# Output projection of a decoder layer: the first three heads' weight blocks by seven block products, in a written-out order

## The chip, the cores and the metric

The kernel runs on one core of one Trainium2 chip. The time is device microseconds (us) from launch to end, the median of several runs. TensorE (PE) does the matrix products; VectorE (DVE), ScalarE (ACT) and GpSimd (POOL) work element by element; SyncE (SP) and ACT start transfers (DMA) between DRAM and on-chip memory.

## The reference

One decoder layer over 512 tokens of width 1024. A matrix-memory attention of four heads (256 columns each) and a causal convolution of width 31 give two halves of 1024 columns, which one output projection maps back; a gated convolutional feed-forward follows. The part that the change touches:

```python
h = mlstm_chunkwise(q, k, v, i_gate, f_gate)            # 4 heads x 256
h = rms_norm(h, ml_norm_g) * sigmoid(o_pre)
y = silu(layer_norm(causal_dwconv(a * sigmoid(gt))))    # 1024 channels
mix = concatenate([h, y], axis=-1) @ w_out[l]           # (512, 2048) @ (2048, 1024)
x = x + g1 * rms_norm(mix, mix_post_g[l])
u = rms_norm(x, ffn_pre_g[l]) * (1.0 + sc2) + sh2
```

All is float32. `sc2`, `sh2` and the gains come from 48 blocks of a conditioning product (`ada_w`).

## The kernel before, in words

**How a product is made.** Each float32 operand is split into a high part, rounded to the matmul's type, and a low part, the rest. `mm3` (the matmuls at L210) then takes three matmuls of 512 columns: high by high, high by low, low by high. Weights come by SP into two raw buffers of 128x2048 (`raws`, RAWS = 2); `w_split` makes the high part on ACT (L191) and the low part on POOL (L192), into 20 tiles (`wpool`, ten pairs). A raw buffer is loaded again when its last split is done, a pair when its last matmul is done.

**The stages.** The input projection, attention head by head (`attention`, with `make_vo` and `head_proj` of the next head between its steps), the output projection, the feed-forward up (`up`) and down (`dn`). The 31 convolution taps run on DVE beside the first half of the program. PE and SP follow the program text; for DVE, ACT and POOL a scheduler sets one order per engine, and each engine then takes its instructions strictly in that order. Inside `in_order()` their order is the program's too.

**The output projection.** 2048 rows of `w_out` are 16 row blocks of 128, of which two belong to each head (`hy[0]` to `hy[7]`) and eight to the convolution (`hy[8]` to `hy[15]`); 1024 columns are two halves of 512; 512 tokens are four tiles. `mix_first` adds the left half into four banks (`mixa`), block by block, between the steps of the last head's attention: scores `s` (L551), sums over values `o` (L562), a factor per token (`ssq`, `fac`, L576 to L581), scaled rows `hn` on ACT (L585), transposed as `hT` (L593), split into `hh` and `hl` (L599, L600). The right half goes into `mixb`: eight blocks for all tiles, and eight in `mix_last`, tile by tile. There a chain per token tile (`chain_sums`, `chain_x`, `chain_u`: L724 to L984) makes the normed row `un`, which PE transposes (`xT`, L992) for the up projection.

**Beside it.** `ada_block` (L176) loads 512 KB from the ACT queue and reduces it on DVE to one column of `mod` (tile `junk`); blocks 24 to 39 use four buffers in `spare` and two in `adas`, and give `sc2` and `sh2`, whose rows `gs2r` and `sh2r` the chain needs. A load into a used buffer waits, on ACT's own queue, for the DVE reduction that read it.

Of the kernel before, what the change touches and what calls it, by code (L numbers as in the profile page):

```python
# [22 lines left out]
H = 4  # L23
# [28 lines left out]
MIX = [*range(6), *range(8, 14), 6, 7, 14, 15]  # L52
# [3 lines left out]
def decoder_layer(ctx, tc, w_glu0, x, c, adaT, vecs, w_glu, w_qko, w_v0, w_vo, w_out, w_up, w_down, out):  # L56
# [111 lines left out]
    def ada_block(i, behind):  # L168
# [5 lines left out]
        nc.scalar.dma_start(r, adaT[i // 2][:, (i % 2) * D : (i % 2 + 1) * D])  # L174
# [51 lines left out]
    def rms_bcast(ps, n, scale, name, bank=atbank):  # L226
# [5 lines left out]
        return bcast(r, n, f"{name}_b", bank)  # L232

    def rms_factor(acc, n, scale, name):
        return rms_bcast(colsum(acc, n, f"{name}_s"), n, scale, name)
# [197 lines left out]

    def glu_gate(i):
# [55 lines left out]
    def make_vo(h):  # L490
# [50 lines left out]
    last_e = [None]  # L541

    def attention(h):
# [35 lines left out]
        G.tensor_tensor(out=fac, in0=ssq, in1=mhalf, op=ALU.pow)  # L579
# [9 lines left out]
        for e in range(2):  # L589
# [99 lines left out]
    def send_rows(a, n, queue=nc.scalar):  # L689
# [3 lines left out]
        t = (side if a == 3 * KT else slot)(f"gTs{a}")[:, :P]  # L693
# [38 lines left out]
    KA = 8  # L732

# [15 lines left out]

# [64 lines left out]
    def norm_mean():  # L814
# [7 lines left out]
        for j in range(KT):  # L822
            V.scalar_tensor_tensor(out=ys[j], in0=tot, scalar=-1.0 / D, in1=ys[j], op0=ALU.mult, op1=ALU.add)

    yr = []

    def norm_sums():
        yr.append(colsum(ysq, T, "ry_s", cvbank))

    def norm_rows():  # L830
        yr.append(rms_bcast(yr[0], T, 1.0 / D, "ry", cvbank))

    def norm_tiles(a, b):
        yb = yr[1]
        for j in range(a, b):
            V.tensor_tensor(out=ys[j], in0=ys[j], in1=yb, op=ALU.mult)
            S.activation(ys[j], ys[j], AF.Silu, bias=vcol("cv_ln_b", j), scale=vcol("cv_ln_g", j))
            hi, lo = slot(f"yh{j}", F32R), slot(f"yl{j}", F32R)
            S.activation(hi, ys[j], AF.Copy)
            V.tensor_tensor(out=lo, in0=ys[j], in1=hi.bitcast(F32), op=ALU.subtract)  # L840
            hy[KT + j] = (hi, lo)

    for h in range(H - 1):
        head_load(h + 1)
        steps = attention(h)
        if h == 0:
# [47 lines left out]

    tc.cur_priority += LATER
    for i in range(16, 20):
        ada_block(i, scaled)
    tc.cur_priority -= LATER
    wo = {}
    steps = attention(H - 1)  # L900
    next(steps)
    mix_first(0)
    next(steps)
    tc.cur_priority += LATER
    for i in range(20, 24):
        ada_block(i, last_e[0])
    ada_done(16, 24)
    gain(0, 16, "mix_post_g")
    tc.cur_priority -= LATER
    norm_rows()  # L910
    norm_tiles(0, 4)
    mix_first(1)
    mix_first(2)
    mix_first(3)
    mix_first(4)
    next(steps)
    norm_tiles(4, KT)
    mix_first(5)
    next(steps)
    mix_first(6)  # L920
    next(steps)
    for n in range(7, 10):
        mix_first(n)
    for _ in steps:
        pass
    spare.append(upool.tile([P, KT, T], F32, tag="ul", name="spare"))
    for i in range(24, 40):
        ada_block(i, last_lo[0])
    ada_done(24, 40)
    for n in range(10, 2 * KT):  # L930
        mix_first(n)
        if n == 10:
            send_rows(0, KT)
    mg = [slot(f"mg{tt}") for tt in range(NT)]
# [4 lines left out]
    for tt, ps in enumerate(mixa):  # L939
        V.tensor_tensor(out=mg[tt], in0=ps, in1=g1r[0], op=ALU.mult)  # L940
        sq_sum(ps, msq[:, 2 * tt : 2 * tt + 1], f"mixa{tt}")
    banks = [atbank(f"mixb{tt}") if tt < 2 else cvbank(f"mixb{tt}") for tt in range(NT)]
    for n_, k in enumerate(MIX[:KA]):
        if n_ % 4 == 0:
            wo = wo_rows(1, n_ // 4)
        for tt, ps in enumerate(banks):
            mm3(ps, (hy[k][0][:, tok(tt)], hy[k][1][:, tok(tt)]), wo[n_ % 4], n_ == 0, False)
# [431 lines left out]
```

## Time and profile before

| | |
|---|---|
| three runs | 769.36, 768.62, 769.15 us; median 769.15 us |
| span of the profiled execution (first to last instruction) | 767.4 us |
| median run less that span | 1.75 us |
| busy share of the span | PE 99%, DVE 75%, POOL 67%, ACT 54% |
| granted TensorE clock, mean | 0.999 |
| output projection, from the first `mixa` matmul to the last of `mixb` | 317.24 to 414.00 us |

The profile is one execution recorded by the hardware. A row of a timeline or of a chain begins with the start in us from the span's beginning and the duration; matmuls overlap, so that their pitch is smaller than their duration. "Idle before" is the time for which the engine had nothing to do, with what ended it. ACTq and SPq are the queues that start transfers.

### The profile page before, as it was taken

The page shows a single profiled execution, that of the slowest core. Times are in us where ns is not written, and L with a number is a line of the kernel's source. Part 1 is how long each engine was busy: PE and PEld are TensorE (multiplying, and loading weights), DVE is VectorE, ACT ScalarE, POOL GpSimd, SP SyncE. Part 2 cuts the span into 40 slices and gives each one's busy share as a digit, 9 for nine tenths or more (in the row PEclk, how much of TensorE's full clock was granted, in tenths as well). Part 3 has the DMA queues.
Part 4 walks back from the last instruction along what each step waited for, and adds up shares of the span by engine and source line. Part 5 has one row for each costly group of instructions (what it writes and reads, how often), then busy time and mean ns, then how long its engine had stood idle before and what let it go on. Part 6 is the DMA issues. An engine that isn't in the chain of part 4 may idle for free.

```text
span 767.4 us, 10129 instructions
## 1 busy us (share of the span) xinstructions
PE 756.0 (99%) x3480; PEld 625.1 (81%) x3480; DVE 576.6 (75%) x837; ACT 410.7 (54%) x778; POOL 516.5 (67%) x428
## 2 busy tenths in 40 slices
PE   7999999999999999999999999999999999999996
PEld 5778898878788788888889988888888888888885
DVE  6669999979979696476989978675684775654547
ACT  6675428585665655573345444443534444566633
POOL 4779849796494872645631179786887884599943
PEclk9999999999999999999999999999999999999999
DMA  8973313411131241655965755666767565796273
GB/s 317 349 281 113 112 56 117 158 56 56 55 111 56 98 168 64 235 199 168 365 222 183 271 210 191 240 219 247 262 231 275 187 239 185 271 397 241 93 249 135
DMA packets 40136, 147.32 MB, mean 192 GB/s; under 512 B 3826, under 2 KB 5266, under 8 KB 30484
## 3 DMA queue, kind: packets, MB, share of 16 engines
q1 hardware_dynamic: 27524, 96.59, 34.9%
q10 hardware_dynamic: 12560, 50.08, 18.3%
q8 instruction: 27, 0.44, 0.2%
q14 instruction: 25, 0.20, 0.1%
HBM read 126.59 MB, written 20.07 MB: 191 GB/s over the span
## 4 chain that ended last, share of the span: by engine, by line
PE 93%; DMA 4%; POOL 1%; ACT 1%; issue 0%; DVEq 0%; SPq 0%; DVE 0%; POOLq 0%; ACTq 0%
PE up L210 31%; PE dn L210 13%; PE qko L210 13%; PE vo L210 9%; PE glu L210 7%; PE mixa L210 6%; PE mixb L210 6%; DMA wglu<-in_w_glu 3%; PE o L562 2%; PE s L551 2%; PE v L210 2%; PE glu L350 1%; DMA xn<-in_x 1%; PE xT L992 0%; PE hT L593 0%
## 5 line engine op out<-in xcount | busy, mean ns | idle before, releaser
L774 DVE SCALAR_TENSOR_TENSOR cv<-gt,cvw,cv 128x485 f32<-128x485 f32 (+24 forms) x200 | 137.2, 731 | 2.1 <-ACT cv L762 0.8
L770 POOL TENSOR_TENSOR cs<-cs,cs 128x510 f32<-128x510 f32 (+3 forms) x32 | 42.1, 1316 | 0.2
L192 POOL TENSOR_TENSOR wup_0l<-wup,wup_0h 128x512 fp32r<-128x512 f32 x18 | 25.0, 1389 | 19.4 <-ACT wup_0h L191 19.3
L210 PE MATMUL up<-u2h,wup_0h 128*128 128x512 f32 (+1 forms) x96 | 35.8, 373 | 0.0
L210 PE MATMUL up<-u2h,wup_0l 128*128 128x512 f32 (+1 forms) x96 | 35.7, 371 | 0.0
L210 PE MATMUL up<-u2h,wup_512h 128*128 128x512 f32 (+1 forms) x96 | 35.6, 371 | 0.0
L210 PE MATMUL up<-u2l,wup_512h 128*128 128x512 f32 (+1 forms) x96 | 35.6, 371 | 0.0
L210 PE MATMUL up<-u2h,wup_512l 128*128 128x512 f32 (+1 forms) x96 | 35.6, 371 | 0.0
L210 PE MATMUL up<-u2l,wup_0h 128*128 128x512 f32 (+1 forms) x96 | 35.6, 371 | 0.0
L210 PE MATMUL up<-u2h,wup_1024h 128*128 128x512 f32 (+1 forms) x92 | 35.0, 381 | 0.0
L210 PE MATMUL up<-u2l,wup_1024h 128*128 128x512 f32 (+1 forms) x92 | 34.9, 380 | 0.0
L210 PE MATMUL up<-u2h,wup_1536l 128*128 128x512 f32 (+1 forms) x92 | 34.9, 380 | 0.0
L210 PE MATMUL up<-u2h,wup_1536h 128*128 128x512 f32 (+1 forms) x92 | 34.9, 380 | 0.0
L210 PE MATMUL up<-u2l,wup_1536h 128*128 128x512 f32 (+1 forms) x92 | 34.9, 380 | 0.0
L210 PE MATMUL up<-u2h,wup_1024l 128*128 128x512 f32 (+1 forms) x92 | 34.9, 380 | 0.0
L176 DVE SCALAR_TENSOR_TENSOR junk<-ada,cb 128x1024 bf16<-128x1024 f32 x20 | 29.9, 1493 | 2.6 <-DMA ada<-in_adaT 2.5
L768 ACT ACTIVATE cs<-gt,cvw 128x511 f32<-128x511 f32 (+4 forms) x40 | 27.1, 713 | 6.1 <-POOL cs L770 3.5
L192 POOL TENSOR_TENSOR wup_1536l<-wup,wup_1536h 128x512 fp32r<-128x512 f32 x18 | 24.6, 1365 | 6.0 <-ACT wup_1536h L191 5.4
L191 ACT ACTIVATE wup_512h<-wup 128x512 fp32r<-128x512 f32 x22 | 13.8, 629 | 25.7 <-PE up L210 20.9
L192 POOL TENSOR_TENSOR wup_1024l<-wup,wup_1024h 128x512 fp32r<-128x512 f32 x18 | 23.6, 1314 | 5.0 <-ACT wup_1024h L191 5.0
L330 DVE SCALAR_TENSOR_TENSOR junk<-ada,cps 128x1024 bf16<-128x1024 f32 x16 | 19.5, 1220 | 9.8 <-DMA ada<-in_adaT 9.2
L1113 DVE TENSOR_TENSOR b<-b 128x512 f32<-128x512 f32 x11 | 19.4, 1762 | 8.6 <-POOL b L1112 8.6
(1097 smaller groups left out, 2726.8 us busy)
## 6 DMA issues: line engine op xcount, KB each, us to landing
wup<-in_w_up SPq DMA_DIRECT2D x22, 1024.0 KB, 5.0
b<-in_w_down ACTq DMA_DIRECT2D x11, 1024.0 KB, 5.1
spill_t<-b ACTq DMA_DIRECT2D x11, 1024.0 KB, 3.9
ada<-in_adaT ACTq DMA_DIRECT2D x20, 512.0 KB, 4.8
wqko<-in_w_qko SPq DMA_DIRECT2D x9, 1024.0 KB, 4.8
ada<-in_adaT SPq DMA_DIRECT2D x16, 512.0 KB, 7.5
wo<-in_w_out SPq DMA_DIRECT2D x8, 1024.0 KB, 5.5
wvo<-in_w_vo SPq DMA_DIRECT2D x6, 1024.0 KB, 4.8
```

The lines of the kernel that those rows point to most:

```text
L176: t = V.scalar_tensor_tensor(out=junk, in0=r, scalar=1.0, in1=cb, op0=ALU.mult, op1=ALU.mult, accum_out=mod[:, i : i + 1])
L191: S.activation(hi[:, :n], src, AF.Copy)
L192: (eng or G).tensor_tensor(out=lo[:, :n], in0=src, in1=hi[:, :n].bitcast(F32), op=ALU.subtract)
L210: PE.matmul(ps, l, r, start=start and i == 0, stop=stop and i == 2, skip_group_check=again)
L330: V.scalar_tensor_tensor(out=junk, in0=first[k][:, i * D : (i + 1) * D], scalar=1.0, in1=cps, op0=ALU.mult, op1=ALU.mult, accum_out=part[: ...
L350: PE.matmul(ps, blk(wk, i)[a], u[k][b], start=k == 0 and p == 0, stop=k == KT - 1 and p == 1)
L551: PE.matmul(sp[:, :n], ks[d][:, cc * P : (cc + 1) * P], qs[d][:, cc * P :], start=d == 0, stop=d == 1)
L562: PE.matmul(o[:, : DH + 2], E[h][cc][:, a : a + P], vs[h][cc], start=cc == 0, stop=cc == tt)
L768: S.activation(t[:, d:], cvx[j][:, : T - d], AF.Copy, scale=w(CK - 1 - d))
L770: G.tensor_tensor(out=side[:, d:], in0=side[:, d:], in1=t[:, d:], op=ALU.add)
L774: tap = V.scalar_tensor_tensor(out=cp[:, d:], in0=cvx[j][:, : T - d], scalar=w(CK - 1 - d), in1=cp[:, d:], op0=ALU.mult, op1=ALU.add)
L1113: V.tensor_tensor(out=b22, in0=b22, in1=b11, op=ALU.subtract)
```

## The change

**Seven products.** The six row blocks of heads 0 to 2 leave the plain sum and become three pairs (`PAIRS = 3`): block 2h against 2h+1, tokens 0 to 255 against 256 to 511, left columns against right. In place of the eight block products of a pair stand seven, over sums of quarters: "11", "12", "s2", "s3", "22" (or "s4" with another weight), "s1", each over 256 tokens, 512 columns and three pairs (`mix_product`). Ten blocks stay plain (`PLAIN`, the convolution first, head 3 last). In `mixa` and `mixb` 384 matmuls become 366.

**Left sums.** For each of the three heads `left_parts` makes, from the scaled rows `y`, the split quarters and the sums of quarters on POOL and ACT: six POOL operations (four of 128x256, two of 128x512) and four ACT copies per head, later one more split each; the two DVE operations `hl` per head go.

**Weight sums.** The weights of the three pairs lie in DRAM as `w_mq` (four quarters of 768 KB). SP copies each into `mixq` (DRAM to DRAM) beside the first projection; four transfers issued by POOL then add one array to another in DRAM: two after the factor of head 0, one each after those of heads 1 and 2.

**Order.** In heads' last round the token tiles 2 and 3 of `make_vo` are interleaved by weight. The stage with the products, and the start of the right half, stand in `in_order`: splits of `m11`, `m21`, `mt2`, `mt3`, `mt4`, copies of unfinished banks (`kept`: one on ACT, one on DVE), the convolution's norm in pieces. The loads of blocks 24 to 27 are put behind the last of these copies on ACT (`load_behind`). `up_split(1)` is done twice ahead of the first chain, and not four times. Loads by SP in the stage become 13, of 512 KB to 1 MB, in place of eight of 1 MB.

The rows below are each engine's instructions in their order. First, DVE before, from the sums of the last head to the first reductions: `dm` to `fac` are the factor per token, `junk` the `ada_block` reductions.

```order
L574 TENSOR_TENSOR dm_3231<-dm_3231,em 128x4
L575 RECIPROCAL rd_3314<-dm_3231 128x4
L569 SCALAR_TENSOR_TENSOR hn_1_3233<-so_1_2869,hn_1_3233 128x512
L576 SCALAR_TENSOR_TENSOR ssq_3230<-ssq_3230,rd_3314 128x4
L577 TENSOR_TENSOR ssq_3230<-ssq_3230,rd_3314 128x4
L581 TENSOR_TENSOR fac_3315<-fac_3315,rd_3314 128x4
L600 SCALAR_TENSOR_TENSOR hl_0_3387<-hT_0_3381,ghalf,hh_0_3386 128x512
L600 SCALAR_TENSOR_TENSOR hl_1_3396<-hT_1_3390,ghalf,hh_1_3395 128x512
L176 SCALAR_TENSOR_TENSOR junk_3401,mod<-spare,cb 128x1024
```

The same place on DVE after the change, where two reductions stand ahead of these rows already.

```order
L649 TENSOR_TENSOR dm_3357<-dm_3357,em 128x4
L181 SCALAR_TENSOR_TENSOR junk_3571,mod<-spare,cb 128x1024
L650 RECIPROCAL rd_3448<-dm_3357 128x4
L644 SCALAR_TENSOR_TENSOR hn_1_3359<-so_1_2904,hn_1_3359 128x512
L181 SCALAR_TENSOR_TENSOR junk_3574,mod<-spare,cb 128x1024
L651 SCALAR_TENSOR_TENSOR ssq_3356<-ssq_3356,rd_3448 128x4
L181 SCALAR_TENSOR_TENSOR junk_3578,mod<-ada_3576,cb 128x1024
L652 TENSOR_TENSOR ssq_3356<-ssq_3356,rd_3448 128x4
L181 SCALAR_TENSOR_TENSOR junk_3582,mod<-ada_3580,cb 128x1024
L197 TENSOR_TENSOR mt_2l<-mt_3659,mt_2h 128x512
L181 SCALAR_TENSOR_TENSOR junk_3585,mod<-spare,cb 128x1024
L181 SCALAR_TENSOR_TENSOR junk_3588,mod<-spare,cb 128x1024
```

The next row is `fac`. Before, no reduction stood between the last head's sums and its `hl`; now eight of the sixteen, and one weight split, stand ahead of `fac`.

ACT after the change, at the scaling of the last head's rows by that factor (`hn` from `hn`); the rows are shown with what each waits for. Before, the four scalings followed the split of a weight.

```order
L176 DMA spare<-in_adaT 128x1024 [waits DMAHW2_49,DVE_49]
L196 ACTIVATE mt_0h<-mt_3659 128x512 [waits DMAHW4_49,Pool_49]
L196 ACTIVATE mt_1h<-mt_3659 128x512
L176 DMA ada_3596<-in_adaT 128x1024 [waits DVE_49]
L196 ACTIVATE mt_2h<-mt_3659 128x512 [waits Pool_49]
L176 DMA ada_3600<-in_adaT 128x1024 [waits DVE_49]
L176 DMA spare<-in_adaT 128x1024 [waits DMAHW3_49,DVE_49]
L176 DMA spare<-in_adaT 128x1024 [waits DMAHW5_49,DVE_49]
L660 ACTIVATE hn_0_3358<-hn_0_3358,fac_3449 128x256 [waits DVE_49]
```

The loads of `ada_block` that wait for a DVE reduction now stand ahead of the scalings on ACT's queue.

SP before, from the right half's last weights (the four `wo` rows) to the second load of the up projection.

```order
L199 DMA wo_0_3573<-in_w_out 128x2048
L199 DMA wo_1_3639<-in_w_out 128x2048
L199 DMA wo_2_3708<-in_w_out 128x2048
L199 DMA wo_3_3726<-in_w_out 128x2048
L954 DMA x_0_3552<-in_x 128x512 x4
L954 DMA x_1_3553<-in_x 128x512 x4
L199 DMA wup_3754<-in_w_up 128x2048
L1009 DMA wup_3772<-in_w_up 128x2048
```

The same after the change; `mt` is the weight of "s1", `m` that of "s4", `wo_8` the last two plain blocks of the left half, and the three `wo` rows at L1106 the right half.

```order
L841 DMA mt_3659<-mixq_616 128x1536
L825 DMA wo_8_3661<-in_w_out 128x1024
L1106 DMA wo_0_3705<-in_w_out 128x1024
L841 DMA m_3715<-in_w_mq 128x1536
L1106 DMA wo_2_3765<-in_w_out 128x2048
L1106 DMA wo_6_3827<-in_w_out 128x2048
L204 DMA wup_3850<-in_w_up 128x2048
L1145 DMA x_0_3654<-in_x 128x512 x2
L1198 DMA wup_3870<-in_w_up 128x2048
```

With two raw buffers each load waits for the splits of the load two ahead of it: the second `wup` for those of `wo_6`, that for those of `m`.

The diff, cut to what the prediction speaks of:

```diff
-MIX = [*range(6), *range(8, 14), 6, 7, 14, 15]
+PLAIN = [*range(8, 16), 6, 7]
+NP = len(PLAIN)
+PAIRS = 3
...
+    def mix_copy(n):
+        q, a = ((1, 0), (3, 1), (2, 3), (4, 2))[n]
+        nc.sync.dma_start(mixq[q], w_mq[a])
...
+    def left_parts(h, e, y):
...
+        x = halfy.pop(h)
+        hi, lo = slot(f"mh{h}", F32R), slot(f"ml{h}", F32R)
+        S.activation(hi, y, AF.Copy)
+        minus(lo, y, hi.bitcast(F32))
+        z["12"], z["22"] = (hi, lo, 0), (hi, lo, HT)
+        z["14"], z["23"] = a, b = slot(f"ms14_{h}"), slot(f"ms23_{h}")
+        minus(a[:, :HT], x[:, HT:], y[:, HT:])
+        minus(b[:, :HT], a[:, :HT], x[:, :HT])
+        minus(b[:, HT:], x[:, :HT], x[:, HT:])
+        G.tensor_tensor(out=a[:, HT:], in0=y[:, :HT], in1=b[:, :HT], op=ALU.add)
+        sums_split(h, "23", (slot(f"ms23h{h}", F32R), slot(f"ms23l{h}", F32R)))
...
+    def mix_add(q, src):
+        tc.cur_priority += LATER
+        behind(G.dma_start(mixq[q], src, accum_op=ALU.add, max_dma_last_dim=2048), last_fac[0])
+        tc.cur_priority -= LATER
...
+    def mix_product(which, w, banks, p, start=False):
+        hi, lo, off = left[p][which]
+        for q, ps in enumerate(banks):
+            ts = slice(off + q * P, off + (q + 1) * P)
+            mm3(ps, (hi[:, ts], lo[:, ts]), w[p], start and p == 0, p == PAIRS - 1, True)
...
+        for p in range(PAIRS):
+            mix_product("s3", wt3, high, p)
+        ku3 = kept(high, "mku3")
+        for i in range(2):
+            wo_split(rw, 0, i)
+        next(steps)
+        norm_silu(6, KT)
+        norm_split(4, KT)
+        for i in range(2, 4):
+            wo_split(rw, 0, i)
+        for p in range(PAIRS):
+            mix_product("22", wt4, high, p)
+        next(steps)
     mix_first(0)
     next(steps)
...
+    for n in range(1, 6):
         mix_first(n)
+    spare.append(upool.tile([P, KT, T], F32, tag="ul", name="spare"))
     for _ in steps:
         pass
...
+        ada_block(i, last_yl[0], last_kept[0] if i < 28 else None)
...
+        wt1 = right_split(wt1)
+        for p in range(PAIRS):
+            mix_product("s1", wt1, banks[:2], p, True)
...
+        for t, ps in zip(ku3, banks):
+            V.tensor_tensor(out=t, in0=ps, in1=t, op=ALU.subtract)
+        for t, ps in zip(ku2, banks):
+            V.tensor_tensor(out=ps, in0=ps, in1=t, op=ALU.subtract)
+        we = wo1_split(wo1_load(0, EARLY), 0, EARLY)
+        w22 = right_split(right_load(w_mq[3], "m22"), slots, "t")
...
+        wo = wo1_split(wo1_load(EARLY, EARLY + 4), EARLY, EARLY + 4)
...
+        for p in range(PAIRS):
+            mix_product("s4", w22, banks[:2], p)
...
+        wo += wo1_split(wo1_load(EARLY + 4, NP), EARLY + 4, NP)
...
         for tt in range(2):
             mix_last(tt, 0, LAST)
-        for _ in range(4):
+        for _ in range(2):
             up_split(1, raw1, slots, "t")
         r = chain_sums(0)
         r = chain_x(0, r)
+        up_split(1, raw1, slots, "t")
         x1_store(0)
```

More of the change, by code (lines that the diff above doesn't have):

```diff
@@ L541, in decoder_layer, with minus, sums_split, urgent @@
     last_e = [None]
+    last_fac = [None]
+    HT = T // 2
+    left = [{} for _ in range(PAIRS)]
+    halfy = {}
+    def minus(out, a, b, eng=G):
+        return eng.tensor_tensor(out=out, in0=a, in1=b, op=ALU.subtract)
+    def left_parts(h, e, y):
+        z = left[h]
+        if e == 0:
+            halfy[h] = y
+            a11 = slot(f"ma{h}", F32R)
+            S.activation(a11[:, :HT], y[:, :HT], AF.Copy)
+            minus(a11[:, HT:], y[:, :HT], a11[:, :HT].bitcast(F32))
+            z["11"] = a11[:, :HT], a11[:, HT:], 0
+            return
+        x = halfy.pop(h)
[13 more added lines that the diff above has]
+        tc.cur_priority -= LATER
+    def sums_split(p, which, home):
+        src = left[p].pop(which)
+        hi, lo = home
+        S.activation(hi, src, AF.Copy)
+        minus(lo, src, hi.bitcast(F32))
+        for n, q in enumerate(which):
+            left[p][f"s{q}"] = hi, lo, n * HT
+    @contextmanager
+    def urgent():
+        tc.cur_priority -= LATER
+        yield
+        tc.cur_priority += LATER
     def attention(h):
@@ L578, in attention @@
         G.tensor_scalar(out=ssq, in0=ssq, scalar1=EPS, scalar2=None, op0=ALU.add)
-        G.tensor_tensor(out=fac, in0=ssq, in1=mhalf, op=ALU.pow)
+        last_fac[0] = G.tensor_tensor(out=fac, in0=ssq, in1=mhalf, op=ALU.pow)
         if h == H - 1:
@@ L897, in decoder_layer @@
         ada_block(i, scaled)
+    for i in range(20, 24):
+        ada_block(i, last_mean[0])
+    ada_done(16, 24)
+    gain(0, 16, "mix_post_g")
     tc.cur_priority -= LATER
@@ L900, in decoder_layer @@
     steps = attention(H - 1)
-    next(steps)
+    low, high = mixa[:2], mixa[2:]
+    s14 = upool.tile([P, KT, T], F32R, tag="uh", name="ms14")
+    norm_factor()
+    w11 = right_split(right_load(w_mq[0], "m11"))
+    w21 = right_split(right_load(w_mq[2], "m21"))
+    wt2 = right_split(right_load(mixq[2], "mt2"))
+    with in_order():
+        next(steps)
+        mix_product("11", w11, high, 0, True)
+        mix_product("11", w11, high, 1)
+        wt3 = right_load(mixq[3], "mt3")
+        next(steps)
+        mix_product("11", w11, high, 2)
+        k1 = kept(high, "mk1")
+        mix_product("12", w21, low, 0, True)
+        norm_rows()
+        norm_scale(0, 4)
+        wt3 = right_split(wt3)
+        wt4 = right_load(mixq[4], "mt4")
+        norm_silu(0, 4)
+        for p in range(PAIRS):
+            mix_product("s2", wt2, high, p)
+        ku2 = kept(high, "mku2")
+        norm_scale(4, KT)
+        wt4 = right_split(wt4)
+        rw = wo_load(0, 4)
+        norm_split(0, 4)
+        mix_product("12", w21, low, 1)
+        mix_product("12", w21, low, 2)
+        for t, ps in zip(k1, low):
+            V.tensor_tensor(out=ps, in0=ps, in1=t, op=ALU.add)
+        norm_silu(4, 6)
+        for p in range(PAIRS):
[3 more added lines that the diff above has]
+            wo_split(rw, 0, i)
+        next(steps)
+        norm_silu(6, KT)
[4 more added lines that the diff above has]
+            mix_product("22", wt4, high, p)
+        next(steps)
@@ L902, in decoder_layer @@
     mix_first(0)
     next(steps)
[L904 to L922, printed above, removed]
+    for p in range(PAIRS):
+        sums_split(p, "14", (s14[:, 2 * p, :], s14[:, 2 * p + 1, :]))
@@ L933, in decoder_layer @@
             send_rows(0, KT)
+    banks = [atbank(f"mixb{tt}") if tt < 2 else cvbank(f"mixb{tt}") for tt in range(NT)]
     mg = [slot(f"mg{tt}") for tt in range(NT)]
```

191 lines of the change are left out of this document (133 added, 58 removed).

## The prediction

> **What bounds the kernel now.** I read the page first, then the chain that ended last, then the timelines of DVE, ACT, POOL and SP from 313 to 404 us. The page:
>
> ```profile
> PE 756.0 (99%) x3480; PEld 625.1 (81%) x3480; DVE 576.6 (75%) x837; ACT 410.7 (54%) x778; POOL 516.5 (67%) x428
> PE 93%; DMA 4%; POOL 1%; ACT 1%; issue 0%; DVEq 0%; SPq 0%; DVE 0%; POOLq 0%; ACTq 0%
> ```
>
> PE is busy for 756.0 us and carries 93% of the chain: whatever it gains or waits shows in the end. The chain through the stage, in order of time (start, us, what):
>
> ```profile
> 317.24 2.73 PE mixa L210 x12
> 333.11 1.31 PE o L562 x6
> 341.20 1.74 PE o L562 x8
> ...
> 354.89 13.64 PE mixa L210 x60
> ...
> 403.37 0.87 PE xT L992 x8
> ```
>
> Piece follows piece: PE waits for nobody, and every factor, weight and row comes in time. So the question is whether they still do when PE's work shrinks and the others' order changes. 60 matmuls in 13.64 us are 227.3 ns each.
>
> **The change part by part: the gain.** 384 matmuls become 366: 18 x 0.2273 = 4.09 us less. With nothing late the profiled execution goes from 767.4 to 763.3, and the median, which lies 1.75 above the span, from 769.15 to 765.06.
>
> **When PE wants the last head's rows.** From 317.24, without waits, at 0.2275 a matmul (2.73 for 12): "11" 2.73, scores 1.31, "11" and "12" 2.73, `ry_b` 0.89 (in the chain between the scores and the sums), "s2" 4.10, "12" 2.73, "s3" 4.10 end at 335.84. Then sums 1.31, "22" 4.10, sums 1.31, `mix_first(0)` 2.73, sums 1.74 and five blocks 13.65: PE reaches `hT` at about 360.7. (`ry_b` row:)
>
> ```profile
> 321.28 0.89 PE ry_b L223 x8
> ```
>
> **What now stands ahead of them.** Before, `fac` follows the sums at once, and the four scalings on ACT follow it; the reductions come later:
>
> ```profile
> 345.44 1.04 POOL L579 TENSOR_TENSOR fac<-ssq,mhalf 128x4 f32<-128x4 f32 x1
> 346.51 1.25 DVE L581 TENSOR_TENSOR fac<-fac,rd 128x4 f32<-128x4 f32 x1 [1.55 <-POOL fac L579]
> 347.79 1.71 ACT L585 ACTIVATE hn<-hn,fac 128x256 f32<-128x256 f32 x4 [1.58 <-DVE fac L581]
> 353.68 1.22 DVE L176 SCALAR_TENSOR_TENSOR junk<-spare,cb 128x1024 bf16<-128x1024 f32 x1
> ```
>
> After, eight reductions and `mt_2l` stand ahead of `fac` on DVE. DVE comes to the first of them when `yl` is done, which waits for ACT's `yh`. ACT's rows have durations in these:
>
> ```profile
> 313.76 1.45 ACTq L174 DMA_DIRECT2D spare<-in_adaT  x3
> 324.61 1.52 ACT L837 ACTIVATE gt<-gt,vec 128x512 f32<-128x512 f32 x2
> 326.03 0.62 ACT L839 ACTIVATE yh<-gt 128x512 fp32r<-128x512 f32 x1
> 326.56 0.61 ACT L191 ACTIVATE wo_1536h<-wo 128x512 fp32r<-128x512 f32 x1
> 340.10 0.15 ACT L565 ACTIVATE dm<-o 128x1 f32<-128x1 f32 x1
> 341.06 0.63 ACT L191 ACTIVATE wo_0h<-wo 128x512 fp32r<-128x512 f32 x1
> ```
>
> Rows follow at 0.53 where the duration says 0.62 (326.03 to 326.56), and a block of sums takes 0.96 (340.10 to 341.06). From 335.84: copy and two splits 1.6, three loads 1.45, two blocks of sums 1.9, one load 0.35, two `gt` 1.42 (324.61 to 326.03), four `yh` 2.1: 344.7, so DVE is free at about 345.
>
> **What eight reductions cost.** Alone a reduction is 1.22 us, a POOL split 1.29. Where both engines have a row of them:
>
> ```profile
> 369.00 1.29 POOL L192 TENSOR_TENSOR wo_0l<-wo,wo_0h 128x512 fp32r<-128x512 f32 x1 [2.27 <-ACT wo_0h L191]
> 377.16 2.28 POOL L192 TENSOR_TENSOR wo_1024l<-wo,wo_1024h 128x512 fp32r<-128x512 f32 x1
> 379.40 2.27 POOL L192 TENSOR_TENSOR wo_1536l<-wo,wo_1536h 128x512 fp32r<-128x512 f32 x1
> 378.33 2.19 DVE L176 SCALAR_TENSOR_TENSOR junk<-spare,cb 128x1024 bf16<-128x1024 f32 x1
> 380.57 2.19 DVE L176 SCALAR_TENSOR_TENSOR junk<-spare,cb 128x1024 bf16<-128x1024 f32 x1
> ```
>
> Both engines step at 2.24 us, nearly the sum of the two: each seems to stand still while the other works. The Trainium skill, "SBUF — State Buffer", section "SBUF: two separate sides", says that DVE and GpSimd share a port pair, held as an exclusive lock for a whole instruction when a DVE operation reads two SBUF inputs and the GpSimd one reads SBUF. By its full sum, 1.22 + 1.29, the eight pairs below would take 2.2 us more; the trace agrees with the rule and puts the pair at 2.24.
>
> From 345 to `fac` POOL has up to eight splits (`wo_2l` to `wo_7l`, `mt_0l`, `mt_1l`). Bounds for DVE: no pairing, 8 x 1.22 = 9.8; full pairing, 8 x 2.24 = 17.9. I take the second, since POOL gets its rows as fast as DVE lets ACT's loads go, which is how the quoted rows came about. With `hn_1` and `mt_2l` (0.65 each, about as a DVE split of that size in the row at 388.60 below), POOL's `fac` 1.04 and three short rows (0.21, as `rm0t` below), `fac` is done at about 366 and the scalings, 1.71, at 367.5. **PE waits 367.5 - 360.7 = 6.8 us at `hT`.** With no pairing: 345 + 9.8 + 1.3 + 1.04 + 0.6 + 1.71 = 359.5, and no wait.
>
> **The second wait.** After `fac` DVE has eight reductions left (9.6), `hl` 1.41, five short rows for `mod` and the gains (0.9), and it stands still for six POOL splits (6 x 1.02, the 2.24 less a reduction): 366 + 18.0, about 384.3 with the gaps. Only then come four subtractions of banks (0.64 each, as `mg` below, which also reads a bank: 386.9), then `m_2l`, the last split of "s4"'s weight (0.65; to 388.5 if POOL's are late). That split frees the raw buffer for `wo_6`, and `wo_6`'s splits free it for the second `wup`:
>
> ```profile
> wo<-in_w_out SPq DMA_DIRECT2D x8, 1024.0 KB, 5.5
> 371.30 1.28 DVE L940 TENSOR_TENSOR mg<-mixa,g1r 128x512 f32<-128x512 f32 x2
> 352.36 1.41 DVE L600 SCALAR_TENSOR_TENSOR hl<-hT,ghalf,hh 128x512 fp32r<-128x512 f32 x2 [4.60 <-ACT hh L599]
> 388.60 0.68 DVE L192 TENSOR_TENSOR wup_0l<-wup,wup_0h 128x512 fp32r<-128x512 f32 x1
> 388.68 0.33 SPq L1009 DMA_DIRECT2D wup<-in_w_up  x1
> 393.58 0.63 ACT L191 ACTIVATE wup_0h<-wup 128x512 fp32r<-128x512 f32 x1 [3.85 <-DMA wup<-in_w_up]
> 396.70 0.21 DVE L724 TENSOR_SCALAR rm0t<-msq 128x1 f32<-128x1 f32 x1
> 400.99 1.42 DVE L984 SCALAR_TENSOR_TENSOR un<-un,rf0r,sh2r 128x512 f32<-128x512 f32 x2 [0.66 <-POOL rf0r L726]
> ```
>
> So: 387.5 to 388.5; `wo_6`, 5.5, to 393 to 394; its high part (0.63) and four splits on POOL (4 x 1.29) to 398.8 to 400.5; `wup`, 4.9 (388.68 to 393.58), to 403.7 to 405.4; and its first two splits (0.63 + 2 x 0.68), which stand ahead of `rm0t` on DVE: 405.6 to 407. From `rm0t` to the end of `un` it is 5.71 now (396.70 to 402.41), so `xT` starts at 411.3 to 412.8, where it starts at 403.37 before. Behind `xT` three of the 18 saved matmuls are still to come (0.68), which may vanish beside the next chain. That is 7.9 to 9.4 later, less 0 to 0.68: **net +7.3 to +9.4 us** for everything behind, which is PE work without a gap. PE itself would come to `xT` at 403.37 less 15 x 0.2275, 400.0, plus the first wait, 406.8; so the first wait lies inside the second and the gain of the matmuls too. I take 7.4, the lower end, since every step was put without a gap that the next one could use and the last row of a chain often has one: span 774.8, median about 776.5. That DVE and POOL keep their places in the row is read from the order; when they come to them is this sum.
>
> **Small things.** The DVE copy of "s3" before "22" has a window of 1.31 us, 0 to 1.3 lost, and the second wait swallows that too. SP's four early copies in DRAM run beside the loads of the first projection:
>
> ```profile
> wglu<-in_w_glu SPq DMA_DIRECT2D x5, 1024.0 KB, 8.0
> ```
>
> If the last of these comes a quarter of its time late, PE loses 2 us; I take 0, since the copies are issued one by one between loads that are two buffers ahead, and leave 0 to 2 in the range.
>
> **Rival one: faster, the waits don't form.** If DVE and POOL do not exclude each other over the whole row of eight (POOL's splits come in time for only a few, or earlier than 345), `fac` comes soon enough. It decides when the scalings end by 360.7 and the subtractions by 375.6 (386.9 less the 11.3 from 400.0 to 411.3). For it: the single rows above at 1.22 with POOL idle. Against: those at 2.19. With all fourteen pairs gone the subtractions end at 384.3 - 14 x 1.02 + 2.6 = 372.6, in time: 765.1. With the first eight alone gone they end at 378.7, 3.1 late: 768; with fewer gone, up to 773. That is the case of partly hidden waits.
>
> **Rival two: POOL's own transfers are dear.** Two additions in DRAM stand behind head 0's factor on POOL, where it is full:
>
> ```profile
> 202.06 1.05 POOL L579 TENSOR_TENSOR fac<-ssq,mhalf 128x4 f32<-128x4 f32 x1
> ...
> 229.94 1.29 POOL L192 TENSOR_TENSOR wvo_1536l<-wvo,wvo_1536h 128x512 fp32r<-128x512 f32 x1
> 234.24 5.47 PE vo L210 x24
> ringuh<-spill_t SPq DMA_DIRECT2D x2, 768.0 KB, 12.2
> ```
>
> The last split there ends at 231.23; PE needs its product 22 matmuls into `vo`, at 234.24 + 5.0 = 239.2. Added: head 0's parts, 4.25 (0.74 a quarter, 1.29 a half), less one row of `cs` moved away, 1.28. That leaves 5.0 us for two issues: it decides at 2.5 each. No POOL transfer is in the trace: bounds 0.33 each (SP's issue, 388.68) and 12.2 (a whole 768 KB transfer between the same queues' ends). I take 0.33 to 1, since what POOL does there is an issue; at 5 each PE loses 5 us there, which nothing behind gives back: 781.5, and 787 at 7.5 each. [...]
>
> **Rival three: the gate.** A wait may cost more than itself: after the last matmul (760.77 + 0.39) the granted clock falls to half within 5 us.
>
> ```profile
> 760.77 0.39 PE L210 MATMUL dn<-p_10h,a_512l 128*128 128x512 f32 x1
> 765.00:766.00 1.00, 0.00 (x0) 0.00 (x0) 0.00 (x0) 0.00 (x0) 0.00 (x0) 0.71 0.86 324
> 766.00:767.40 1.40, 0.00 (x0) 0.00 (x0) 0.00 (x0) 0.00 (x0) 0.00 (x0) 0.50 0.00 0
> ```
>
> 0.71 between a full clock and 0.50 is a fall at about 765.4, 4.3 us after PE stops; a wait of 6.8 crosses that. PE at half speed behind `hT` runs into the second wait anyway, so I add nothing; if a wait at `xT` itself crosses it, the next matmuls lose a few us, inside the range. The Trainium skill, "TensorE: Matmul & The Clock Gate", Part 1, has about 3.4 us of work until full speed returns: an estimate of 1.7 us lost.
>
> **How the numbers follow.** Forecast (both waits): 0.55, 773 to 779. Partly hidden: 0.13, 768 to 773. All hidden: 0.20, about 765. POOL's transfers dear: 0.12, 779 to 787. 0.2%, 1.5 us, is about what a measurement of this kernel can tell from no change: faster under 767.6, slower over 770.7. All hidden and a little of the partly hidden are faster: 0.22; 0.06 in between; 0.72 slower. The range leaves out most of the dear transfers and the lowest tip: 766 to 780; the likeliest case's own is 773 to 779.
>
> **What would show it.** Right: an idle of some 7 us at the last head's `hT` put down to ACT `hn`, the eight `junk` rows ahead of `fac` at about 2.2 us beside POOL splits, the second `wup` issued near 400, `rm0t` near 406, and between `hT` and the first `xT` together some 11 us in which PE has no work. Wrong: `junk` rows at 1.2 there, no PE idle from 342 to 400, a POOL issue over 2.5 us near 203 with PE idle in `vo` near 239, or more matmuls than 3462.

## The result, and the profile after

The changed kernel took 792.71 us (median of 5 runs, 787.15 to 799.77), the kernel before 769.07 (767.77 to 769.36): slower, ratio 1.028 (95% interval 1.0247 to 1.0313). In six later runs of the same kernel it was 796.38 (789.39 to 798.93), ratio 1.0346 (1.0315 to 1.0376). Its times scatter over 12 us where those before stay within 2; the profile below is of one of the longer runs, with a span of 798.1 us, while the first ratio leaves the longer ones out. The profile that was taken later (e10) has the same three longest waits. Forecast were 776.5 and a range up to 780: the side was right, the size three times too small.

The page's first line of the changed kernel, and the start of its chain:

```profile
PE 762.4 (96%) x3462; PEld 628.4 (79%) x3462; DVE 597.8 (75%) x849; ACT 421.7 (53%) x802; POOL 552.9 (69%) x458
PE 65%; DVE 15%; issue 7%; DMA 4%; POOL 4%; ACT 3%; ACTq 0%; SPq 0%; DVEq 0%; POOLq 0%
```

18 matmuls fewer, and PE is busy for 6.4 us more; it carries 65% of the chain and not 93%. The view of PE's waits says who it waited for (us in total, times, longest):

```profile
PE hT L668 <- DVE E L627: 8.4, 1, 8.4
PE o L637 <- ACT hn L641: 5.4, 1, 5.4
PE hT L668 <- ACT hn L660: 4.9, 1, 4.9
PE xT L1182 <- DVE un L1174: 3.1, 1, 3.1
...
PE glu L352 <- ACT uh L373: 1.7, 1, 1.7
PE mixa L215 <- DVE mk L859: 1.7, 1, 1.7
PE mixa L215 <- ACT mku L858: 0.8, 1, 0.8
PE mixa L215 <- POOL mt_0l L197: 0.4, 1, 0.4
```

The rows are, from the top: head 0's transposes, a sum of head 1, the last head's transposes (the forecast's first wait), the first transposes of the next stage (its second), the start, two bank copies between the products, and a weight split. They sum to 26.4 us. (The row left out, 2.9 us ahead of the program's first matmul, is the same before and after.) The same count before gives 2.25:

```profile
PE glu L350 <- ACT uh L371: 1.3, 1, 1.3
PE glu L350 <- ACT uh L405: 0.9, 1, 0.9
```

And behind each long wait the clock is low. Stretches around the end of the first, with PE's busy time in the second column and the granted clock third from the end:

```profile
220.00:222.00 2.00, 0.88 (x4) 0.88 (x5) 1.53 (x4) 0.64 (x2) 1.47 (x2) 0.50 0.67 193
222.00:224.00 2.00, 2.00 (x9) 1.81 (x8) 1.37 (x2) 2.00 (x4) 2.00 (x2) 0.50 0.98 410
224.00:226.00 2.00, 2.00 (x8) 1.58 (x8) 1.08 (x2) 2.00 (x5) 2.00 (x3) 0.77 0.07 25
226.00:228.00 2.00, 2.00 (x11) 1.65 (x10) 1.93 (x4) 2.00 (x5) 2.00 (x3) 1.00 0.00 0
```

PE is busy all of 222 to 226 and gets through 9 and 8 matmuls in 2 us each, where 10 to 12 are usual. Over 1 us windows, PE's busy time times what the clock lacks gives 1.7 us behind the start's wait, then 1.9, 2.4, 2.3 and 1.7 behind the four long ones: 10.0. The account:

| | us |
|---|---|
| span before | 767.4 |
| 18 matmuls fewer | -4.1 |
| waits, 26.4 in place of 2.25 | +24.2 |
| matmuls at the low clock | +10.0 |
| sum; span after | 797.5; 798.1 |

In the other profiles (e7, which adds work, left out) the same sum stays 1.5 to 3.3 us short of the span, so that it closes to 0.6 here is partly luck.

Of the 24.2, 13.8 arise in heads 0 and 1, for which the prediction's sum had nothing. The first one's place on POOL and DVE:

```profile
202.74 1.20 POOL L601 DMA_DIRECT2D mixq<-in_w_mq  x1
210.33 0.97 POOL L601 DMA_DIRECT2D mixq<-in_w_mq  x1 [6.39 <-PE qko L215]
210.96 1.66 POOL L197 TENSOR_TENSOR wqko_1024l<-wqko,wqko_1024h 128x512 fp32r<-128x512 f32 x1
213.87 6.59 DVE L900 SCALAR_TENSOR_TENSOR ydl<-ysum,gt 128x512 f32<-128x512 f32 x1 [9.50 <-POOL gt L894]
220.39 0.68 DVE L627 SCALAR_TENSOR_TENSOR E<-s,E 128x512 f32<-128x512 f32 x1
```

POOL issues two transfers behind the factor, and the second starts 7.6 us after the first, which lands at 210.07. POOL's overdue rows then come in one run, and a DVE row of 0.7 us lasts 6.59 beside them; the scores' row `E`, for which PE waits, stands behind it. The second one, in head 1:

```profile
284.08 1.29 POOL L197 TENSOR_TENSOR wvo_0l<-wvo,wvo_0h 128x512 fp32r<-128x512 f32 x1
284.70 7.54 DVE L181 SCALAR_TENSOR_TENSOR junk<-ada,cb 128x1024 bf16<-128x1024 f32 x1
285.32 1.30 POOL L575 TENSOR_TENSOR ml<-hy,mh 128x512 fp32r<-128x512 f32 x1
...
290.43 0.73 POOL L575 TENSOR_TENSOR ms<-ms,hy 128x256 f32<-128x256 f32 x1
```

Seven POOL rows in a row, at their usual lengths, and one reduction that stands still beside all of them: it ends 1.09 us behind the last. A load on ACT's queue waits for it, three more reductions and their loads follow late, and the copies of the sums stand behind these loads on ACT. Before, the four reductions at this place took 1.22 to 2.27 us, beside POOL rows with gaps between them.

The stage itself went nearly as forecast, some 20 us later. From the timeline, the last factor, the last head's transposes, the last subtractions' begin, the second `wup` and the first chain:

```profile
386.49 0.16 DVE L656 TENSOR_TENSOR fac<-fac,rd 128x4 f32<-128x4 f32 x1
387.55 1.67 PE L668 MATMUL hT<-ident,hn 128*128 128x128 f32 x4 [4.94 <-ACT hn L660]
406.63 1.28 DVE L1121 TENSOR_TENSOR mixb<-mixb,mku 128x512 f32<-128x512 f32 x2
420.14 0.33 SPq L1198 DMA_DIRECT2D wup<-in_w_up  x1
426.94 0.21 DVE L805 TENSOR_SCALAR rm0t<-msq 128x1 f32<-128x1 f32 x1
```

and, from the chain, the transposes that follow:

```profile
432.63 1.77 PE xT L1182 x8
```

From the end of `fac` to the end of the subtractions it is 21.3 us (forecast 366 to 386.9, 20.9); from there to `rm0t` 19.0 (18.7 to 20.1); from there to `xT` 5.69 (5.71).

### The profile page after: what moved, and what is told of

It reads as the page before. It is cut to its first block, busy times and chain, and to the rows that moved or that the text cites. A ratio compares the mean times of both kernels' runs of the same rounds, so it can differ in the third digit from the quotient of the medians.

```text
span 798.1 us, 10177 instructions
## 1 busy us (share of the span) xinstructions
PE 762.4 (96%) x3462; PEld 628.4 (79%) x3462; DVE 597.8 (75%) x849; ACT 421.7 (53%) x802; POOL 552.9 (69%) x458
## 4 chain that ended last, share of the span: by engine, by line
PE 65%; DVE 15%; issue 7%; DMA 4%; POOL 4%; ACT 3%; ACTq 0%; SPq 0%; DVEq 0%; POOLq 0%
PE up L215 30%; PE dn L215 11%; PE glu L215 7%; PE glu L352 4%; PE vo L215 4%; DVE cv L886 4%; PE qko L215 4%; DVE junk L181 3%; PE mixb L215 1%; PE o L637 1%; POOL ms L575 1%; PE v L215 1%; DMA wup<-in_w_up 1%; DMA wglu<-in_w_glu 1%; DVE yl L962 1%
## 5 line engine op out<-in xcount | busy, mean ns | idle before, releaser
L886 DVE SCALAR_TENSOR_TENSOR cv<-gt,cvw,cv 128x502 f32<-128x502 f32 (+23 forms) x200 | 136.7, 729 | 2.0 <-ACT cv L874 0.7
L181 DVE SCALAR_TENSOR_TENSOR junk<-ada,cb 128x1024 bf16<-128x1024 f32 x20 | 35.9, 1793 | 8.0 <-DMA ada<-in_adaT 7.8
L1306 POOL TENSOR_TENSOR b<-b 128x512 f32<-128x512 f32 x11 | 14.7, 1335 | 17.0 <-DVE b L1305 14.1
L637 PE MATMUL o<-v,E 128*128 128x258 f32 x80 | 21.0, 403 | 5.4 <-ACT hn L641 5.4
```

The source lines that it names most:

```text
L181: t = V.scalar_tensor_tensor(out=junk, in0=r, scalar=1.0, in1=cb, op0=ALU.mult, op1=ALU.mult, accum_out=mod[:, i : i + 1])
L637: PE.matmul(o[:, : DH + 2], E[h][cc][:, a : a + P], vs[h][cc], start=cc == 0, stop=cc == tt)
L886: tap = V.scalar_tensor_tensor(out=cp[:, d:], in0=cvx[j][:, : T - d], scalar=w(CK - 1 - d), in1=cp[:, d:], op0=ALU.mult, op1=ALU.add)
L1306: G.tensor_tensor(out=b12, in0=b22, in1=b12, op=ALU.subtract)
```

## The experiments

The theories: **transfers** (POOL's issues hold it up, and its backlog shuts DVE out), **left sums** (their rows alone overfill POOL), **shut-out** (a DVE row with two inputs stands still beside a run of POOL rows), **order of the reductions** (the forecast's), **DVE-full** (its row sets the stage, whatever the order), **gate** (a wait costs a slow stretch too). The changed kernel was at 787 to 800 us.

**e1: no transfers.** One line out; the kernel leaves out the four additions that make the weight sums:

```diff
-        behind(G.dma_start(mixq[q], src, accum_op=ALU.add, max_dma_last_dim=2048), last_fac[0])
+        pass
```

> Leaves out the four additions in DRAM that POOL issues, so four of the seven products get wrong weights; every other row is the changed kernel's. Theory POOL-transfer: the first transfer holds POOL from 202.7 to 210.3 in the changed kernel's trace, the rows behind it then come in one unbroken run that shuts DVE out for 6.6 us, and PE waits 8.4 us at head 0's hT and then runs some 4 us at half clock. Without the transfers that wait and its slow stretch go, 10 to 11 us, and POOL is less late in head 1, which shortens the 5.4 us wait there: about 772 to 779 against 787 to 793. Theory left-sums: POOL is overfull from the added rows of the left sums (4.25 us a head) alone; then the wait at head 0's hT stays above 3 us and the time is 784 to 790.

789.11 us (785.89 to 790.04), ratio 1.0261. The waits:

```profile
PE o L637 <- ACT hn L641: 8.5, 2, 7.3
```

Head 0's wait is gone, as the first theory says. The time is a few us shorter at most, and not at the 772 to 779 expected, for head 1's wait grew from 5.4 to 7.3. The reduction there took 8.43 us beside seven POOL rows: less backlog in head 0 did not relieve head 1.

**e2: the factor first.** 14 of 16 reductions behind the last factor:

```diff
-        ada_block(i, last_yl[0], last_kept[0] if i < 28 else None)
+        ada_block(i, yl_end if i < 26 else last_yl[0], last_kept[0] if i < 28 else None)
```

with `last_yl[0]` set to the factor's DVE row and `yl_end` to what it was before.

> Only the reductions of blocks 26 to 39 are put behind the last head's factor on DVE; the order then also puts the four subtractions and the last split of the weight of s4 ahead of six reductions. Theory order-of-reductions: the 4.9 us wait at the last hT and its slow stretch (2.2 us) go, and the second load of the up weights comes sooner too: about 780 to 783 against 787 to 793, with head 0's and head 1's waits as they were. Rival: DVE is full from 366 to 408 whatever the order, so what is gained at hT is waited at the first xT: 786 to 792.

800.28 us (792.97 to 801.99), ratio 1.0395: the longest median, though its interval (1.0339 to 1.0452) overlaps that of the changed kernel's later runs. The profile is of the shortest of its four runs, 792.97; the others took about 800. The wait at the last `hT` is gone; in its place PE stands at the small transposes of the gains:

```profile
PE gT L772 <- DVE gains L1142: 8.2, 1, 8.2
```

So DVE-full holds in this run: what is put ahead on DVE is paid behind. This run tells something else too: in head 1, beside the same POOL rows, the reduction did not stand still but took turns with POOL,

```profile
284.26 1.74 DVE L181 SCALAR_TENSOR_TENSOR junk<-ada,cb 128x1024 bf16<-128x1024 f32 x1
286.04 2.19 DVE L181 SCALAR_TENSOR_TENSOR junk<-ada,cb 128x1024 bf16<-128x1024 f32 x1
284.87 2.27 POOL L575 TENSOR_TENSOR ml<-hy,mh 128x512 fp32r<-128x512 f32 x1
```

and the wait there was 0.7 us. One place in one order has two outcomes, which fits the scatter of the times but does not show its cause.

**e3: two transfers earlier,** into 17.45 us in which POOL had nothing to do:

```diff
-            mix_add(1, w_mq[1])
-            mix_add(3, w_mq[3])
+            mix_add(1, w_mq[1], side_of[FREE])
+            mix_add(3, w_mq[3], side_of[FREE])
```

> Two of the four additions, those behind head 0's factor, are issued ahead of it, where POOL had nothing to do for 17.45 us (184 to 201 us); nothing is left out. Theory POOL-transfer: two issues of some 7.6 us fit there, so the wait at head 0's hT and its slow stretch go: 776 to 781. Theory left-sums: that wait stays above 3 us: 785 to 791. If an issue takes more than 8.7 us the splits of the next weights come late and PE waits ahead of 203 us instead.

791.48 us (789.51 to 791.56), ratio 1.0299. Head 0's wait is gone and head 1's is 7.3, as in e1. The second issue again stood until long after the first, where it delays nobody:

```profile
181.31 1.15 POOL L601 DMA_DIRECT2D mixq<-in_w_mq  x1
189.82 0.97 POOL L601 DMA_DIRECT2D mixq<-in_w_mq  x1 [7.36 <-issue]
```

**e4: reductions 16 to 19 later.**

```diff
     for i in range(16, 20):
-        ada_block(i, scaled)
+        ada_block(i, last_mean[0])
```

> Only the reductions of blocks 16 to 19 move, from beside head 1's left sums to behind the mean of the convolution. Theory shut-out: in the changed kernel one reduction stood still for 7.5 us beside seven POOL rows in a row, ACT's load behind it held up the copies of a sum, and PE waited 5.4 us at a sum; with no reduction there that wait and its slow stretch go: 7 to 8 us, 780 to 784. Rival: another DVE row with two inputs is shut out by the same POOL rows, or the four reductions delay the splits at the start of the output projection by as much: 786 to 792.

793.97 us (790.46 to 798.47), ratio 1.0335. Head 1's wait is gone, head 0's stays, but the time is not shorter than the changed kernel's by more than its scatter. Both halves of the rival are there. Another DVE row, `hn`, stood 5.19 us beside POOL rows in head 1, though PE did not wait for it. And the four reductions now stand ahead of the bank copies, where PE waits 4.5 us in place of 2.5 and a low stretch of the clock costs 3.1 that the changed kernel does not have: 5.1 of the 7.8 us won are gone again.

```profile
PE hT L668 <- DVE E L627: 8.6, 1, 8.6
...
PE mixa L215 <- ACT mk L858: 2.7, 1, 2.7
```

**e5: e3 and e4 together.**

> Both moves together: two of POOL's transfers go into its idle stretch and the reductions of blocks 16 to 19 behind the convolution's mean; nothing is left out. Alone, the first took the 8.5 us wait at head 0's hT away and the wait at a sum of head 1 stood at 7.3 us, and the second took that one away and the first stood at 8.6. Theory: they are two waits of their own, of which one run of the changed kernel has either one or both; then the span is 787.8 (first move alone) less 7.3, less some 2 us at half clock behind it, plus 1 to 2.4 us more at the bank copies ahead of s2: 779 to 781, the time 780 to 783. Rival: another DVE row is shut out by a run of POOL rows and the time stays at 786 to 792.

786.11 us (784.66 to 787.47), ratio 1.0219 (1.0202 to 1.0236). Both long waits are gone, and the runs lie within 3 us of each other. But 3 to 6 us less were saved than expected:

```profile
PE mixa L215 <- ACT mk L858: 4.0, 1, 4.0
PE hT L668 <- ACT hn L660: 3.2, 1, 3.2
PE xT L1183 <- DVE un L1175: 3.1, 2, 2.2
...
PE mixa L215 <- ACT mku L858: 1.9, 1, 1.9
```

12.9 us of waits in all, and 8.6 lost to a low clock behind four waits of 1.9 to 4.0 us. The clock follows a rule that can be read from the traces. Within each of them every fall and rise lies on one grid of 3.41 us: the five falls in the changed kernel are 197.97, 85.33, 85.33 and 47.79 us apart, 58, 25, 25 and 14 times 3.413, and a low stretch lasts 3.41 us or two to four times that. Here are two windows of such grids, each with the one that follows; the first pair is of e5 and holds its wait of 1.9 us, the second is of the changed kernel and holds a wait of 1.66 (PE's busy time in the second column, the clock third from the end):

```profile
343.68:347.09 3.41, 1.52 (x7) 0.97 (x6) 2.73 (x5) 1.12 (x2) 0.68 (x1) 1.00 0.81 298
347.09:350.50 3.41, 3.41 (x9) 2.63 (x9) 0.69 (x1) 3.22 (x11) 1.88 (x2) 0.50 0.86 263
...
344.38:347.79 3.41, 1.75 (x8) 1.37 (x8) 3.41 (x7) 1.43 (x3) 3.41 (x4) 1.00 0.26 32
347.79:351.20 3.41, 3.41 (x17) 2.83 (x16) 2.75 (x6) 2.36 (x4) 0.89 (x1) 1.00 0.82 252
```

PE had no work for 1.89 us of the first window and for 1.66 of the third; behind the first the clock is at half for a window, behind the third it is not. In all twelve traces, from 10 us on, a window at full clock with 1.98 us or more without PE work is followed by half clock, and one with 1.70 or less never is; of the six windows between (1.73 to 1.90 us) four are.

**e6: eight splits from POOL to DVE,** on e5:

```diff
-        wo[n + i] = w_split(r[:, i * T : (i + 1) * T], f"wo0_{n + i}")
+        wo[n + i] = w_split(r[:, i * T : (i + 1) * T], f"wo0_{n + i}", eng=V if n + i > 3 else G)
...
-        wt1 = right_split(wt1)
+        wt1 = right_split(wt1, on_v=0)
```

> The kernel of both moves, and eight splits that stood on POOL beside the reductions (the last six plain blocks of the left half and two of the weight of s1) are made on DVE; nothing is left out. Theory two-engines-exclude: a reduction beside a POOL split costs DVE 1.02 us more, and a split on DVE 0.62; taking POOL out of that stretch frees 3 to 4 us ahead of the last head's factor, POOL's factor is 1 us shorter, so the wait at the last hT falls from 4.4 to 4.8 us to under 1.5 and no slow stretch follows: 5 us less than the kernel of both moves, up to 2 given back at the first xT: 774 to 778 where that one is at 780 to 783. Rival: the rows are late for another reason (ACT, the loads), the wait stays above 3.5 us, and the time is that of both moves or more.

782.87 us (780.49 to 784.63), ratio 1.0181 (1.0158 to 1.0204): 3.2 us less than e5 in one and the same comparison, where 5 were expected. DVE's rows agree with the reason given:

```profile
366.04 0.69 DVE L197 TENSOR_TENSOR mt_0l<-mt,mt_0h 128x512 fp32r<-128x512 f32 x1 [1.92 <-ACT mt_0h L196]
366.65 0.68 DVE L197 TENSOR_TENSOR mt_1l<-mt,mt_1h 128x512 fp32r<-128x512 f32 x1
367.25 1.22 DVE L181 SCALAR_TENSOR_TENSOR junk<-ada,cb 128x1024 bf16<-128x1024 f32 x1
```

With POOL silent a reduction is 1.22 us, and a split that POOL made at a cost of 1.02 to DVE costs DVE 0.6 if it makes it itself. The wait at the last `hT` fell to 2.2 and not below 1.5: DVE now stands 1.92 us for the weight of "s1", whose load a raw buffer holds back.

**e7: four filler products** ahead of the last transposes, on e5:

```diff
+            for _ in range(4 if h == H - 1 and e == 0 else 0):
+                PE.matmul(tp, ident, cb[:, :T], start=True, stop=True)
```

> The kernel of both moves, with four products of 128x512 float32 ahead of the last head's transposes, into the bank that the transposes then fill: work of no use, about 3.4 us, within the wait of 4.4 to 4.8 us. Theory gate: the granted clock falls after about 3 us without work and is half for some 4 us after it; with PE busy it stays at 1.00 there and 2 us are saved against the kernel of both moves. Rival: the clock doesn't matter here because the next wait, at the first xT, swallows it: the same time within 1 us, and the wait at xT 2 us longer.

788.95 us (788.44 to 790.11), ratio 1.0264. No wait is left at `hT`, and the clock stays at 1.00 there,

```profile
374.00:376.00 2.00, 2.00 (x6) 0.71 (x5) 2.00 (x4) 0.60 (x2) 0.61 (x1) 1.00 0.86 258
```

where e5 has 0.60. That much of the gate theory holds. But PE then waits 5.48 us at the gains' transpose, for `hl` on DVE, and the clock falls behind that one: the rival's swallowing, at another place than it said, and 2.8 us worse.

**e8: one transfer early, one behind head 0's factor.**

> Of the two transfers behind head 0's factor only one stays there; the other goes into POOL's idle stretch some 20 us earlier. Nothing is left out. Theory second-behind-first: an issue itself takes POOL 1.0 to 1.2 us, and it was the second one that stood until the first had landed (7.2 us); then POOL's next split follows the factor within 3 us, and head 0's hT waits under 1 us. Rival, each issue holds POOL some 7 us: the next split starts 7 us or more behind the factor and hT waits 5 us or more. The time is 785 to 792 either way by whether head 1's wait of 5 to 7 us is there; the two rows decide.

793.38 us (two runs), ratio 1.0326. An issue alone takes 1.1 us:

```profile
181.35 1.11 POOL L601 DMA_DIRECT2D mixq<-in_w_mq  x1
182.26 1.54 POOL L197 TENSOR_TENSOR wqko_0l<-wqko,wqko_0h 128x512 fp32r<-128x512 f32 x1
202.80 1.08 POOL L601 DMA_DIRECT2D mixq<-in_w_mq  x1
203.53 1.68 POOL L197 TENSOR_TENSOR wqko_1024l<-wqko,wqko_1024h 128x512 fp32r<-128x512 f32 x1
```

So it was the second of two in a row that stood, until the first had landed. The traces bear this out: in the nine profiles that have two in a row the second starts 7.6 to 9.8 us behind the first, and each time 0.26 us behind its landing. The PE matmul that the row at 210.33 names was done at times that vary, 0.36 to 0.67 us earlier, and in five of the nine none is named. Head 0's wait is 1.0 us, though a DVE row stands still there too, 8.67 us beside six POOL rows. So what cost PE 8.4 us in the changed kernel was that the second transfer put this run of POOL rows 7.4 us later. Head 1's wait was 10.5 in this run, with a reduction of 9.67 us beside nine POOL rows.

**e9: short reductions,** on e3; 24 reductions are copies of one column, so the modulation is left out:

```diff
+        if 16 <= i < 40:
+            t = V.tensor_copy(mod[:, i : i + 1], r[:, :1])
```

> The kernel of the early transfers (787.8 us span), in which the 24 reductions of blocks 16 to 39 are copies of one column: every load, wait and place in the order stays, DVE's 1.2 to 2.3 us for each falls to some 0.1, and the modulation of the layer is not the reference's. Theory DVE-full: from 317 us on DVE's row sets the waits at the bank copies, the last hT and the first xT; with some 40 us taken out of it, the 7.3 us wait in head 1, the 4.4 us one at hT and the one at xT go, with their slow stretches, under 3 us of waits are left at the bank copies, and the saved 4.1 us come through: 765 to 769, against 768.8 before the change. Rival: the weight chain (two raw buffers, splits on POOL and ACT) is too long by itself: the waits at xT or in the mixb matmuls stay above 4 us and the time is 772 to 780.

768.74 us (10 runs, 768.03 to 770.18), ratio 1.0005 (0.9996 to 1.0015): no difference from the kernel before.

```profile
PE o L640 <- ACT hn L644: 1.2, 1, 1.2
PE gT L775 <- DVE hl L683: 1.1, 1, 1.1
PE glu L355 <- ACT uh L376: 0.8, 1, 0.8
PE xT L1186 <- DVE un L1178: 0.7, 1, 0.7
```

All long waits and, up to the last matmul, all slow stretches are gone, with every load, transfer, left sum and split still there: the weight chain is not too long by itself. Some 20 us of the changed kernel's loss hang on DVE's reductions; how much of that is their own time and how much what they lose beside POOL, this run does not separate. The 4.1 us saved do not come through, though. With `mixa` and `mixb` ahead of the first `xT` PE is busy for 78.2 us (330 matmuls) in place of 80.7 (345): 2.5 us saved there and not 3.4. The waits that are new, 1.2, 1.1, 0.7 and 0.3, take about as much.

**e10: the changed kernel again.**

> The changed kernel itself, once more: its first profile was of a run of 798.1 us, while others took 785 to 791. Theory one-or-both: the wait at head 0's hT (8.4 us) is in every run, and the one at a sum of head 1 (5.4 us and some 2 us at half clock) only in some, by whether a reduction there is shut out by POOL's run or takes turns with it; a run of 786 to 791 us then shows the first at 8 to 9 us and the second under 1.5, and its waits at the bank copies, the last hT and the first xT are as before. Rival: the shorter runs have both waits, and the difference lies in the transfers or in the clock of another stretch.

796.38 us; six runs at 798.93, 795.21, 789.39, 797.54, 797.94 and 794.36. The profile is of a run of 797.2 us span and has both long waits, 8.75 and 5.48 us; a shorter run was not profiled. The theory is neither shown nor refuted by it; that these rows can run without the second wait is shown by e2 alone, in another order.

## Why the prediction was wrong

- **The bound and the gain.** PE was the bound, and 18 matmuls less were right. That they are worth 4.09 us was a little too much: e9 shows 2.5 of 3.4 us where the waits are left out. Why is not shown.
- **No term for the POOL rows added in heads 1 and 2.** This step failed. I priced the left sums' POOL rows only in head 0, and there only against PE's need of one split; in heads 1 and 2 they stood at nothing, without a reason. There are seven of them a head, five of 128x256 and two of 128x512. What the runs showed: in head 1 POOL ran without a gap, with four left sums among the seven rows, and beside such a run a DVE reduction took 7.5 to 9.7 us. Price: 5.4 us of waiting and 2.4 at the low clock. e4 took that wait away by moving the reductions alone. That the left sums closed POOL's gaps is read from the rows; no run leaves them out.
- **"I take 0.33 to 1, since what POOL does there is an issue."** This step failed as well. An issue was 1.0 to 1.2 us, near what I took, but the second of two stood until the first had landed, 7.6 us. That lies over the 5.0 us of slack and inside the bound of 12.2 that I had and did not take. Price: 8.4 us and 1.9. The rival had the row on POOL right. It had the wait elsewhere, in `vo` near 239 for a split; PE waited at head 0's `hT`, at 221, for DVE's `E`. And its mechanism, an issue that is dear by itself, is refuted by e8.
- **The first wait, 6.8 us,** was 4.9, by the mechanism named, though not row by row: of the eight reductions ahead of `fac` four took 2.2 to 2.3 us and four 1.2, beside which `dm`, `hn_1` and the two `ssq` rows stood still instead (1.24 to 1.68 us, where they take 0.15 to 0.69). The rest is PE, which came to `hT` 1.3 us later against `fac` than forecast (two bank copies made it wait 2.5 us, where I had 0 to 1.3), and `hT`, which began 0.9 us behind `fac` and not 1.5. The Trainium skill's rule of the shared port pair ("SBUF — State Buffer", section "SBUF: two separate sides") agrees with the pairs at 2.2. What that page of the Trainium skill calls the loser's full block was, in head 1, a block over seven to nine POOL instructions and not over one.
- **The second wait** had its three terms right within 1 us (21.3 for 20.9, 19.0 for 18.7 to 20.1, 5.69 for 5.71); the upper ends of its sum are a little high (394 and 5.79 make 399.8, not 400.5). From `hT` to `xT` it was 45.1 us, forecast 43.8 to 45.3. Of the 4.5 to 6.0 us that PE was then to wait at `xT`, 3.1 were left, since 2.3 had gone to the low clock behind `hT`.
- **"PE at half speed behind `hT` runs into the second wait anyway, so I add nothing."** Behind `hT` this held, as just said. It failed for the kernel as a whole: five slow stretches, 10.0 us, four of them behind waits that I had not priced or behind `xT`. I read from the end of the program that the clock falls 4.3 us after the last matmul, and took that for the length that a wait must have. The changed kernel shows a fall behind a wait of 1.7 us, e5 one behind 1.9. The Trainium skill, "TensorE: Matmul & The Clock Gate", Part 1, says that the gate looks at windows of about 3.4 us that run on by themselves; the traces agree, with their grid of 3.41 us. The same part of the Trainium skill has the clock fall after an idle window, and here a window without work for little more than its half was enough (1.73 of 3.41 us); the measurement decides.
- **"Rival one: faster, the waits don't form"** would have needed DVE's row shorter. e9 makes it so by leaving most of the reductions' work out, and the result is no change, not faster.

What stays open: what decides whether a DVE row takes turns with POOL's rows (e2) or is shut out by all of them. The reductions of e2 and of the changed kernel both start 0.6 us behind the begin of a POOL row. A run without gaps is not enough: before, four scalings in head 0 took turns with five POOL rows in a run, at 1.36 us each. No run separates the two cases. Which waits the shorter runs of the changed kernel lack was not profiled either.

## What to carry to other kernels

Where PE has no wait, look at the engine that will be next before counting matmuls: here DVE's busy time rose by 21 us and POOL's by 36, standing still beside each other included, and the kernel lost six times what PE was to save. Price a change of order over every stage that its side products touch, not only at the stage that it rewrites, and give each wait of 2 us and more another 1.6 to 3.1 for the clock, as these traces show it. When POOL must issue transfers, put a gap as long as a landing between two, and put them where POOL has nothing to do.

## What the runs showed of the hardware that was not expected

- A DVE row can be shut out by a run of POOL rows until the run ends: a row of 0.7 us took 6.59 beside five, reductions of 1.22 took 7.54 beside seven and 9.67 beside nine, and in e8 a scaling that reads one array, 0.40 alone, took 8.67 beside six. The shut-out reductions end 1.08 or 1.09 us behind the last POOL row. In other places such rows take turns, at 2.2 us a pair.
- The second of two transfers issued in a row by POOL (768 KB each, 384 rows of 2 KB) started 7.6 to 9.8 us behind the first, 0.26 us after its landing in all nine profiles, and POOL did nothing meanwhile; one alone took 1.1 us and POOL's next row followed at once.
- The granted clock changes on a grid of 3.41 us. It fell to half at the end of a window in which PE had been without work for more than about half, which a wait of 1.7 or 1.9 us can do, up to 1.6 us after PE was at work again. Each fall behind such a wait cost 1.6 to 3.1 us.
